# Query projections ahead of attention: a ring of five weight pairs, a rope table in scratch memory, three more query pairs made before the first score

## The chip, the core and the metric

One Trainium2 chip; the kernel runs on one of its cores. The metric is the device time of one execution in microseconds (us). Engines are named as in the profile: PE multiplies matrices, DVE works on vectors, ACT casts and applies functions, POOL works on vectors and issues DMAs, SP issues DMAs.

## The reference

A trunk of two layers over 1024 latent tokens and 256 context tokens, width 1024. Layer 0 mixes tokens with a convolution module, layer 1 with grouped-query attention; a SwiGLU feed-forward network (FFN) follows each. The changed part is the attention's input:

```python
qx = apply_rope(rmsnorm((hx @ wq).reshape(B, S, N_HEADS, HEAD_DIM), q_g), cos, sin)
kx = apply_rope(rmsnorm((hx @ wk).reshape(B, S, N_KV_HEADS, HEAD_DIM), k_g), cos, sin)
vx = (hx @ wv).reshape(B, S, N_KV_HEADS, HEAD_DIM)
...
s = jnp.einsum("bqkgd,bskd->bkgqs", qg, k).astype(jnp.float32) * (Dh ** -0.5)
p = jax.nn.softmax(s, axis=-1).astype(v.dtype)
o = jnp.einsum("bkgqs,bskd->bqkgd", p, v)
```

There are 16 query heads and 4 key heads of 64 each. Keys and values are those of 1024 latent and 256 context tokens, 1280 in all.

## The kernel before, in words

**Split operands.** Float32 products are made of halves: each operand is split in hi (rounded to float32r) and lo (the rest), and a product is three matmuls: hi with hi, lo with hi, hi with lo. For a weight of 128 x 1024 this is done in `wload` (L134 to L148): SP loads it (L141), ACT casts hi (L142), DVE (L146) or POOL (L148) subtracts lo; `lo_dve` sets the share of the two. The halves lie in pools of three, `wh` and `wl`, so a fourth weight's cast waits until the oldest one has been used up. The raw weights have buffers of their own (`wr0`, `wr1`, and room in `q`).

**Thirds.** The 1280 tokens are worked in three pieces: context (C), left latent (L, 512 tokens) and right latent (R, 512). The FFN of layer 0 is first run on C and L, then on R; as background of the latter the key and value of C are made. PE's products of two weights share the lines L165 to L167, or L176 to L178 for a first operand that is worked k by k.

**Projections for layer 1.** `qkv` (L802) is a generator that makes for one piece a key pair (hLk, hRk), values, and four query pairs (qL0 to qL3, qR0 to qR3). A pair is two 128-row results of 512 tokens, the even and odd halves of a rope rotation; `qk_pair` (L748 to L800) handles it. ACT squares both (L764, L765) and copies them scaled (L766, L767) into E and O, of which there are two sets, used in turn; PE sums the squares (L772, 16 small matmuls), DVE takes the reciprocal root (L775, L329 to L337). DVE then rotates: L790 writes both products with sin into `t12`, of which there is one, L791 to L793 do the rest. ACT casts the hi half into `t12` (L797) and POOL stores it from there to DRAM (`qsd`, L836; a key to `ksd`, L813); DVE makes the lo half in E and O (L799), and POOL stores that. A key has the root spread by PE (L783, L787) and multiplied in (L795) besides. All of it lies in the buffer `self.wk`, tile T5 of 4096 numbers a partition. The tables of cos and sin are loaded at the start of each `qkv` by two DMAs of POOL (L808, L809), for the left piece into HS.

In the order of the program: qkv of L begins (hLk, qL0, ...) as background work, beside it the last norm of FFN(0) on R and the first of layer 1 (L624, L627, L395, L401, on DVE, with sums on PE, L349, L363, L375); then hRk, qR0, and the rest of L. Which background step comes when is set by estimated costs (`pump`); a scheduler then orders each engine's queue, and every engine runs its own in that order.

**Attention.** Units are pairs of key head and tile of 128 queries, four query heads each. `scores` (L858 on) has PE write 128 x 1280 scores (L870), DVE scale them into one of several probability slots and take the minimum (L876), ACT exponentiate (L878). `values` transposes on PE (L888), casts (L891) and subtracts (L892) halves, ten times a unit, and multiplies by values (L894, L895). The first 16 units are for left queries (tiles 0 to 3), the next 16 for right ones. At the start of attention, three query pairs of the right piece are still to be made. They run as background of the first units; for as long, the score area has one place (`sring = [TOK]`) and two banks serve the projections. When they are done, T5 becomes three more probability slots and the score area has two places:

```python
for us in self.attn_stream(units, (self.kub, kbuf), dst(0), True):
    if self.bgq:
        self.pump(self.rate * us)
    elif pr4 is None:
        pr4 = self.T("T5", [P, 3, TOK])
        self.pring = self.pring[:4] + [pr4[:, 0], pr4[:, 1], pr4[:, 2]] + self.pring[4:]
        self.set_banks(**alone)
        self.sring = [0, TOK]
```

A tile such as T5 or HS, allocated anew, waits for all reads and stores of what lay there. In attention HS holds four probability slots (`prh`, "score area"); ahead of it, it holds the last operands of FFN(0) and then the table of the left piece, 1024 numbers of some 5120 a partition.

Of the kernel before, what the change touches and what calls it, by code (L numbers as in the profile page):

```python
# [8 lines left out]
F32 = mybir.dt.float32  # L9
F32R = mybir.dt.float32r  # L10
# [5 lines left out]
P = 128  # L16
# [3 lines left out]
SEQ = 1024  # L20
# [4 lines left out]
NH, NKV, HD = 16, 4, 64  # L25
# [29 lines left out]
class Kern:  # L55
    def __init__(self, tc, es, a):
        self.tc, self.nc, self.a = tc, tc.nc, a
        ep = es.enter_context
        self.cp = ep(tc.tile_pool(name="const", bufs=1))
        self.tp = ep(tc.tile_pool(name="sets", bufs=1))  # L60
        self.wp = ep(tc.tile_pool(name="w", bufs=3))
        self.sp = ep(tc.tile_pool(name="scr", bufs=3))
        self.pp = ep(tc.tile_pool(name="ps", bufs=1, space=bass.MemoryType.PSUM))
        self.dp = ep(tc.tile_pool(name="dr", bufs=1, space=bass.MemoryType.DRAM))
        self.ps = self.pp.tile([P, 8, 512], F32, tag="ps", name="ps")
        self.ring = {}
        self.set_banks(mm=[0, 1, 2], md=[3], st=[5, 6], cv=[4, 7])
        self.raws = [self.wp.tile([P, 1024], F32, tag=f"wr{i}", name=f"wr{i}", bufs=1) for i in range(2)]
        self.ri = 0
        self.bgq = []  # L70
        self.tie = None
        self.pre = []
        self.pace = 1
        self.rate, self.credit = 1.0, 0.0
        self.qk = 0
        self.share, self.lo_dve = 0.0, 0.0
# [58 lines left out]
    def wload(self, ap):  # L135
        nc = self.nc
        n = int(np.prod(ap.shape[1:]))
        raw = self.raw()[:, :n]
        hi = self.wp.tile([P, 1024], F32R, tag="wh", name="wh")[:, :n]
        lo = self.wp.tile([P, 1024], F32R, tag="wl", name="wl")[:, :n]  # L140
        nc.sync.dma_start(raw if len(ap.shape) == 2 else raw.rearrange("p (a b) -> p a b", a=ap.shape[1]), ap)  # L141
        nc.scalar.copy(hi, raw)  # L142
        self.share += self.lo_dve
        if self.share >= 1:
            self.share -= 1
            nc.vector.tensor_tensor(lo, raw, hi.bitcast(F32), op=ALU.subtract)  # L146
        else:
            nc.gpsimd.tensor_tensor(lo, raw, hi.bitcast(F32), op=ALU.subtract)  # L148
        return hi, lo
# [48 lines left out]
    def consts(self):  # L198
        nc, a = self.nc, self.a
        c = self.c = {}  # L200
        n = sum(int(np.prod(v)) for _, v in CONST)
        cst = self.cp.tile([P, n], F32, tag="cst", name="cst")
        nc.scalar.dma_start(cst, a["cst"])
        o = 0
        for k, v in CONST:
            w = int(np.prod(v))
            c[k] = cst[:, o:o + w]
            if len(v) > 1:
                names = "abc"[:len(v)]
                c[k] = c[k].rearrange("p (%s) -> p %s" % (" ".join(names), " ".join(names)), **dict(zip(names, v)))  # L210
            o += w
        self.x1d = a["x1d"] if "x1d" in a else self.dp.tile([P, KT, TOK], F32, tag="x1d", name="x1d")
        self.x2d = a["x2d"] if "x2d" in a else self.dp.tile([P, KT, TOK], F32, tag="x2d", name="x2d")
        self.x3d = a["x3d"] if "x3d" in a else self.dp.tile([P, KT, SEQ], F32, tag="x3d", name="x3d")
        self.qsd = a["qsd"] if "qsd" in a else self.dp.tile([NKV, P, 4, SEQ], F32, tag="qsd", name="qsd")
        self.ksd = a["ksd"] if "ksd" in a else self.dp.tile([NKV, HD, 2, TOK], F32, tag="ksd", name="ksd")
        self.od = self.dp.tile([P, KT, SEQ], F32, tag="od", name="od")

        self.vc = [self.dp.tile([CG, P, NC_], F32, tag=f"vc{k}", name=f"vc{k}") for k in range(KT)]
        self.vl = [self.dp.tile([CG, P, NL], F32, tag=f"vl{k}", name=f"vl{k}") for k in range(KT)]  # L220
        cs = self.cp.tile([P, KT, 2], F32, tag="cs", name="cs")
# [580 lines left out]
    def qkv(self, h, col0, n, wk, rope=None):  # L802

        nc, a, c = self.nc, self.a, self.c
        x = self.pairs(*h)
        lat0 = col0 - CTX
        if rope is not None:
            nc.gpsimd.dma_start(rope[:, 0, :n], a["cos"][:, lat0:lat0 + n])  # L808
            nc.gpsimd.dma_start(rope[:, 1, :n], a["sin"][:, lat0:lat0 + n])  # L809

        def ksink(i, v):
            for e in range(2):
                nc.gpsimd.dma_start(self.ksd[:, 32 * e:32 * e + 32, i, col0:col0 + n], v[:, e])  # L813
        pe, po = self.bank("mm"), self.bank("mm")
        self.projs((pe, po), a["wk"], x, n)
        self.qk_pair(pe, po, n, c["kg"], rope, wk, ksink)
        yield 5.0
        wv = [self.wload(a["wv"][q]) for q in range(2)]
        for j in range(n // P):
            out = self.bank("mm")  # L820
            self.mm3(out,
                     self.pairs(*h, j * P, (j + 1) * P),
                     lambda k: tuple(w[:, (k % 4) * 256:(k % 4 + 1) * 256] for w in wv[k // 4]),
                     KT, 256)
            jj = col0 // P + j
            ov = out[:, :256].rearrange("p (h d) -> p h d", d=HD)
            vh, vl = self.vst[:, :, jj, 0:HD], self.vst[:, :, jj, HD:P]
            nc.scalar.copy(vh, ov)
            nc.vector.tensor_tensor(vl, ov, vh.bitcast(F32), op=ALU.subtract)
            yield 0.5  # L830
        if rope is not None:
            for t in range(NKV):
                def qsink(i, v):
                    for e in range(2):
                        r = 64 * i + 32 * e
                        nc.gpsimd.dma_start(self.qsd[t, r:r + 32, :, lat0:lat0 + n].rearrange("d h t -> h d t"),  # L836
                                            v[:, e])
# [107 lines left out]
    def build(self):  # L945
        nc, a, c = self.nc, self.a, None
        self.consts()
        c = self.c
        hs = {b: [] for b in PIECES}
# [154 lines left out]
        def early():  # L1104
            yield from final(0, zv["C"][0], self.x1d, self.x2d, *PIECES["C"], 0, "KB")
            yield from final(0, zv["L"][0], self.x1d, self.x2d, *PIECES["L"], 0, "KB")
            yield from self.norm_in(1, None, (None, "T2", "T2"), 0, CTX, hC, xt=zv["C"][0][0])
            self.vst = self.T("HR", [P, NKV, NJ, P], F32R)
            self.rq = [self.cp.tile([P, SEQ // P * 4], F32, tag=f"rq{t}", name=f"rq{t}") for t in range(NKV)]
            wk = self.T("KB", [P, 8, 256])  # L1110
            yield from self.qkv(hC[0], 0, CTX, wk)
            yield from self.norm_in(1, None, (None, "T3", "T2"), CTX, CTX + 512, hL, xt=zv["L"][0][0])
            self.wk = self.T("T5", [P, 8, 512])
        self.raws.append(self.room())
        self.set_banks(mm=[0, 1, 2, 3], st=[5, 6], cv=[4, 7])
        self.bgq.append(early())
        for us in self.ffn(0, [(fv["R"][0], 512)], ("T1",), ("HS",), (zv["R"],)):
            self.pump(0.5 * us)
        self.drain()
        rope = self.T("HS", [P, 2, 512])  # L1120
        self.bgq.append(self.qkv(hL[0], CTX, 512, self.wk, rope))
        self.pump(7)
        self.kub = self.T("KB", [P, 2 * TOK], F32R)
# [6 lines left out]
        qr = self.qkv(hR[0], CTX + 512, 512, self.wk, self.wk[:, 0:2])  # L1130
        next(qr)
        self.load_k(0, self.kub, CTX + 512, TOK)
        for _ in range(5):
            next(qr)
        self.drain()
        self.attention(final, qr)

    def attention(self, final, qr):
        nc, a, c = self.nc, self.a, self.c
# [3 lines left out]
        ptt = self.T("T2", [P, 4, 2, 512], F32R)  # L1143
        self.ptring = [(ptt[:, i, 0], ptt[:, i, 1]) for i in range(4)]
        self.ptslot = self.si = self.qi = 0
        del self.raws[2:]
        self.qroom = self.room()
        units = [(t, q) for t in range(NKV) for q in range(4)]

# [183 lines left out]
```

## Time and profile before

| | us |
|---|---|
| median of 3 runs (3049.22 to 3057.86) | 3055.4 |
| profiled execution | 3058.17 |
| its span | 3056.4 |
| projections, from the last matmul of FFN(0) to the first score read | 1495.8 to 1641.0 |
| three pairs beside attention's first units | 1640 to 1757 |
| one unit of attention alone | 14.7 |

The profile is of one execution. A busy PE is not PE at its peak: matmuls are pipelined, and the bar of one overlaps the next. What a line waits for is named by the profile with the last semaphore that came. A pair's rope line is found by tile T, its store by `qsd`.

### The profile page before, as it was taken

To read this page: it belongs to the slowest core of one execution; us is meant where nothing else is said; L and a number is where in the kernel's file an instruction comes from. 1 tells how busy PE (TensorE), PEld (TensorE's weight loads), DVE (VectorE), ACT (ScalarE), POOL (GpSimd) and SP (SyncE) were. 2 spreads that over 40 slices of the span, in tenths; PEclk is the share of its full clock that TensorE was granted. 3 is DMA by queue.
4 is the path that set the end of the run, shared out by engine and by line. 5 is a ranking of instruction groups with operands and counts; after the bars stand their busy time and mean duration, and the time that the engine had idled before them with its cause. 6 is when DMAs were issued, how large, how long until landed. Compare 5 with 4: busy or idle time off the path is not lost. (4 is left out here: it accounts for less than half of the span.)

```text
span 3056.4 us, 39302 instructions
## 1 busy us (share of the span) xinstructions
PE 2927.2 (96%) x15086; PEld 2438.8 (80%) x15086; DVE 1902.2 (62%) x3341; ACT 1207.4 (40%) x1981; POOL 261.1 (9%) x413
## 2 busy tenths in 40 slices
PE   7899969999999999999988999999999999999997
PEld 5788868888888888888877777777787778788886
DVE  5886777866566358333565899766666654743335
ACT  5222255432222234222333688645555542332222
POOL 0000000101112011000013111110000000100000
PEclk9999979999999999999989999989999999999999
DMA  6542424433346235333346311223223132443332
GB/s 236 147 122 75 122 76 138 159 114 126 119 156 198 67 105 157 105 97 97 126 134 151 88 45 47 92 70 90 72 69 86 58 135 95 148 136 97 97 93 66
DMA packets 140716, 336.96 MB, mean 110 GB/s; under 512 B 39920, under 2 KB 61424, under 8 KB 139376
## 3 DMA queue, kind: packets, MB, share of 16 engines
q1 hardware_dynamic: 76432, 221.94, 22.6%
q0 software_dynamic: 37984, 104.42, 11.5%
q10 hardware_dynamic: 26112, 8.10, 1.1%
q8 instruction: 118, 1.93, 0.3%
q14 instruction: 70, 0.57, 0.1%
HBM read 289.76 MB, written 39.19 MB: 108 GB/s over the span
## 5 line engine op out<-in xcount | busy, mean ns | idle before, releaser
L167 PE MATMUL ps<-T,wl 128*128 128x512 f32 (+1 forms) x2128 | 802.9, 378 | 11.8 <-DVE wl L146 11.8
L165 PE MATMUL ps<-T,wh 128*128 128x512 f32 (+1 forms) x2128 | 806.3, 380 | 6.9 <-ACT T L154 4.1
L166 PE MATMUL ps<-T,wh 128*128 128x512 f32 (+1 forms) x2064 | 777.9, 377 | 0.7 <-DVE T L157 0.7
L142 ACT CAST wh<-wr 128x1024 fp32r<-128x1024 f32 x296 | 310.8, 1050 | 796.8 <-PE ps L166 569.0
L146 DVE TENSOR_TENSOR wl<-wr,wh 128x1024 fp32r<-128x1024 f32 x288 | 352.0, 1223 | 311.5 <-ACT wh L142 307.1
L167 PEld LDWEIGHTS ps<-T,wl 128*128 128x128 f32 x2128 | 407.3, 192 | 85.9 <-DVE wl L146 14.1
L165 PEld LDWEIGHTS ps<-T,wh 128*128 128x128 f32 x2128 | 407.2, 192 | 79.7 <-ACT T L154 5.6
L166 PEld LDWEIGHTS ps<-T,wh 128*128 128x128 f32 x2064 | 395.5, 192 | 68.9 <-DVE T L157 2.0
L166 PE MATMUL ps<-HS,wh 128*128 128x512 f32 (+1 forms) x784 | 303.8, 388 | 0.0
L892 DVE TENSOR_TENSOR T<-ps,T 128x512 fp32r<-128x512 f32 x320 | 216.7, 686 | 110.9 <-ACT T L891 109.7
L167 PE MATMUL ps<-HS,wl 128*128 128x512 f32 (+1 forms) x720 | 278.9, 388 | 0.0
L165 PE MATMUL ps<-HS,wh 128*128 128x512 f32 (+1 forms) x720 | 278.7, 389 | 0.0
L891 ACT CAST T<-ps 128x512 fp32r<-128x512 f32 x320 | 185.9, 585 | 194.8 <-PE ps L888 172.8
L888 PE MATMUL ps<-cst,T 128*128 128x128 f32 x1100 | 192.2, 276 | 1.9 <-DVE T L892 1.8
L876 DVE TENSOR_SCALAR_CACHE_REDUCE T<-ps,rq 128x1280 f32<-128x1280 f32 x110 | 169.9, 1544 | 27.8 <-PE ps L870 23.0
L722 DVE TENSOR_TENSOR T<-ps,T 128x512 f32<-128x512 f32 (+1 forms) x168 | 110.3, 662 | 113.1 <-PE ps L167 112.2
L888 PEld LDWEIGHTS ps<-cst,T 128*128 128x128 f32 x1100 | 134.0, 142 | 49.0 <-DVE T L892 28.6
L878 ACT ACTIVATE T<-T,mn 128x1280 f32<-128x1280 f32 x110 | 150.4, 1367 | 57.1 <-DVE T L876 55.2
L166 PEld LDWEIGHTS ps<-HS,wh 128*128 128x128 f32 x784 | 147.5, 188 | 28.6 <-DVE HS L157 0.2
L697 DVE TENSOR_TENSOR sm<-sm,ps 128x256 f32<-128x256 f32 (+1 forms) x88 | 54.5, 619 | 181.4 <-PE ps L167 181.2
L870 PE MATMUL ps<-KB,q 128*128 128x512 f32 (+1 forms) x576 | 146.8, 374 | 14.2 <-DVE HS L876 9.9
L167 PEld LDWEIGHTS ps<-HS,wl 128*128 128x128 f32 x720 | 135.4, 188 | 27.0
(227 smaller groups left out, 4574.0 us busy)
## 6 DMA issues: line engine op xcount, KB each, us to landing
wr<-in_w SPq DMA_DIRECT2D x220, 512.0 KB, 3.5
q<-in_w SPq DMA_DIRECT2D x44, 512.0 KB, 3.5
wr<-in_pw SPq DMA_DIRECT2D x40, 512.0 KB, 3.6
HR<-in_wmodT POOLq DMA_DIRECT2D x56, 256.0 KB, 3.9
q<-in_wmodT POOLq DMA_DIRECT2D x56, 256.0 KB, 3.9
qsd<-T POOLq DMA_DIRECT2D x32, 256.0 KB, 10.7
q<-qsd POOLq DMA_DIRECT2D x32, 256.0 KB, 3.3
wr<-in_wo SPq DMA_DIRECT2D x16, 512.0 KB, 4.4
```

The lines of the kernel that those rows point to most:

```text
L142: nc.scalar.copy(hi, raw)
L146: nc.vector.tensor_tensor(lo, raw, hi.bitcast(F32), op=ALU.subtract)
L165: nc.tensor.matmul(out[:, :n], lhsT=wh, rhs=xh, start=k == 0, stop=False)
L166: nc.tensor.matmul(out[:, :n], lhsT=wh, rhs=xl, start=False, stop=False)
L167: nc.tensor.matmul(out[:, :n], lhsT=wl, rhs=xh, start=False, stop=k == nk - 1)
L722: nc.vector.tensor_tensor(yd, out[:, :c1 - c0], yd, op=ALU.add)
L870: nc.tensor.matmul(sc[:, k0:k0 + w], lhsT=q[:, h, :], rhs=kt[:, p * TOK + k0:p * TOK + k0 + w], start=p == 0, stop=p == 1)
L876: nc.vector.tensor_scalar(out=pt, in0=sc, scalar1=rq[:, h:h + 1], scalar2=None, op0=ALU.mult, op1=ALU.min, accum_out=mn)
L878: nc.scalar.activation(pt, pt, AF.Exp, bias=mn, scale=-1.0, accum_out=sums[:, 0, h:h + 1])
L888: nc.tensor.transpose(tp[:, h * P:(h + 1) * P], Ps[h][:, j * P:(j + 1) * P], c["ident"])
L891: nc.scalar.copy(ph, tp)
L892: nc.vector.tensor_tensor(pl, tp, ph.bitcast(F32), op=ALU.subtract)
```

## The change

Three edits.

First, the pools of three hi and lo halves become a list of three explicit pairs, `self.whl`, taken in turn by a running count. Behind FFN(0) on R, HS is allocated as five slabs of 1024 numbers; four of them are two more pairs, so the ring has five until attention begins, where it is cut back to three (`del ... self.whl[3:]`). The fifth slab is the rope table of the left piece.

Second, the tables of cos and sin are copied to one scratch tensor in DRAM by two DMAs of POOL, 512 KB each, so that a piece's table of both is one DMA of 512 KB in place of two of 256 KB.

Third, three more steps of the right piece's generator run before attention: qR1, qR2 and qR3 are made there, and the loop above finds no background work but the generator's end.

```diff
-        hi = self.wp.tile([P, 1024], F32R, tag="wh", name="wh")[:, :n]
-        lo = self.wp.tile([P, 1024], F32R, tag="wl", name="wl")[:, :n]
+        self.wi += 1
+        hi, lo = (t[:, :n] for t in self.whl[self.wi % len(self.whl)])
...
+        self.rope = self.dp.tile([P, 2, SEQ], F32, tag="rope", name="rope")
...
-            nc.gpsimd.dma_start(rope[:, 0, :n], a["cos"][:, lat0:lat0 + n])
-            nc.gpsimd.dma_start(rope[:, 1, :n], a["sin"][:, lat0:lat0 + n])
+            nc.gpsimd.dma_start(rope[:, :, :n], self.rope[:, :, lat0:lat0 + n])
...
             self.wk = self.T("T5", [P, 8, 512])
+            for i, t in enumerate(("cos", "sin")):
+                nc.gpsimd.dma_start(self.rope[:, i], a[t])
...
-        rope = self.T("HS", [P, 2, 512])
+        hs = self.T("HS", [P, 5, 1024], F32R)
+        rope = hs[:, 4].bitcast(F32).rearrange("p (i n) -> p i n", i=2)
+        self.whl += [(hs[:, i], hs[:, i + 1]) for i in (0, 2)]
...
         self.drain()
+        for _ in range(NKV - 1):
+            next(qr)
         self.attention(final, qr)
...
-        del self.raws[2:]
+        del self.raws[2:], self.whl[3:]
```

What moves in the queues. In the changed kernel a line behind L800 has a number larger by three, so L790 is L793 there, L142 is L144, L395 is L398 and L876 is L878; the numbers behind names tell allocations apart.

ACT where FFN(0) ends and the projections begin, before; `wh_11486` and `wh_11491` are the first two weights of the projections:

```order
L142 CAST wh_11438<-q_8935 128x1024
L696 ACTIVATE sm_11388<-ps_72 128x512
L142 CAST wh_11486<-wr0_73 128x1024
L154 CAST HS_8937<-sm_11389 128x512
L383 ACTIVATE acc_11394<-T1_8936 128x512
L386 ACTIVATE sb_11415<-T1_8936 128x512
L142 CAST wh_11491<-wr1_74 128x1024
```

The same place in the changed kernel:

```order
L144 CAST wh2_79<-q_8730 128x1024
L699 ACTIVATE sm_11049<-ps_72 128x512
L156 CAST HS_8732<-sm_11050 128x512
L386 ACTIVATE acc_11055<-T1_8731 128x512
...
L144 CAST wh2_79<-wr0_73 128x1024
L389 ACTIVATE sb_11137<-T1_8731 128x512
L144 CAST HS_11140<-wr1_74 128x1024
```

The last weight of FFN(0) lies in `wh2`; the next cast, the first of the projections, goes to `wh2` too, and the second to HS. Both now stand behind the reads of T1 by L389.

DVE at the norm of the right piece, before (L395 and L401 are the norm, L790 begins the rope of qL1):

```order
L337 SCALAR_TENSOR_TENSOR nr<-nq,nr 128x16
L779 TENSOR_SCALAR rq_9471<-nr 128x16
L395 SCALAR_TENSOR_TENSOR sb<-T_8936,col_8057,ps 128x512 x3
L401 SCALAR_TENSOR_TENSOR T_11833<-sb,mod_103,T_11832 128x512 x3
L395 SCALAR_TENSOR_TENSOR sb<-T_8936,col_8057,ps 128x512 x3
L401 SCALAR_TENSOR_TENSOR T_11833<-sb,mod_103,T_11832 128x512 x3
L395 SCALAR_TENSOR_TENSOR sb<-T_8936,col_8057,ps 128x512 x2
...
L790 TENSOR_TENSOR T_9937<-T_9937,HS 128x1024
```

In the changed kernel:

```order
L340 SCALAR_TENSOR_TENSOR nr<-nq,nr 128x16
L793 TENSOR_TENSOR T_9688<-T_9688,HS 128x1024
L398 SCALAR_TENSOR_TENSOR sb<-T_8731,col_7880,ps 128x512 x3
L404 SCALAR_TENSOR_TENSOR T_11481<-sb,mod_110,T_11480 128x512 x3
L398 SCALAR_TENSOR_TENSOR sb<-T_8731,col_7880,ps 128x512 x3
L404 SCALAR_TENSOR_TENSOR T_11481<-sb,mod_110,T_11480 128x512 x3
L398 SCALAR_TENSOR_TENSOR sb<-T_8731,col_7880,ps 128x512 x2
...
L794 TENSOR_TENSOR T_9688<-T_9688,HS 128x1024
```

The first rope product of qL1 stands ahead of the norm, the second still behind it.

DVE at the first scores of attention in the changed kernel, from the first product of qR3 (`T_12498` is T1, `T_12523` is T5):

```order
L793 TENSOR_TENSOR T_9688<-T_9688 128x1024
...
L794 TENSOR_TENSOR T_9688<-T_9688 128x1024
...
L878 TENSOR_SCALAR T_12498,mn<-ps,rq_9244 128x1280
...
L878 TENSOR_SCALAR HS,mn<-ps,rq_9244 128x1280
...
L802 TENSOR_TENSOR T_9688<-T_9688 128x1024
...
L878 TENSOR_SCALAR T_12498,mn<-ps,rq_9244 128x1280
...
L878 TENSOR_SCALAR HS,mn<-ps,rq_9244 128x1280
...
L878 TENSOR_SCALAR T_12523,mn<-ps,rq_9244 128x1280
L901 RECIPROCAL sums<-sums 128x4
L894 TENSOR_TENSOR T_12500<-ps,T_12500 128x512
```

In before the first score (L876) stands between qL2 and qL3, and the four products L790 of qL3, qR1, qR2 and qR3 lie between the scores of the first units; now all of them stand ahead of the first score, and the fifth score is written to T5, where the pairs' buffers lay.

More of the change, by code (lines that the diff above doesn't have):

```diff
@@ L68, in __init__ @@
         self.raws = [self.wp.tile([P, 1024], F32, tag=f"wr{i}", name=f"wr{i}", bufs=1) for i in range(2)]
-        self.ri = 0
+        self.ri = self.wi = 0
+        self.whl = [tuple(self.wp.tile([P, 1024], F32R, tag=f"{t}{i}", name=f"{t}{i}", bufs=1) for t in ("wh", "wl"))
+                    for i in range(3)]
         self.bgq = []
```

## The prediction

> **What bounds the kernel now.** I read the page's totals first, then a table of stretches around the place that changes, then the waits there.
>
> ```profile
> span 3056.4 us, 39302 instructions
> PE 2927.2 (96%) x15086; PEld 2438.8 (80%) x15086; DVE 1902.2 (62%) x3341; ACT 1207.4 (40%) x1981; POOL 261.1 (9%) x413
> ```
> ```profile
> core 0: us, PE busy (x) PEld busy (x) DVE busy (x) ACT busy (x) POOL busy (x), PEclk, DMA share, GB/s
> 5.00:42.00 37.00, 26.82 (x168) 17.68 (x169) 18.43 (x60) 17.10 (x48) 0.00 (x0) 0.86 1.03 399
> 1495.00:1640.00 145.00, 131.61 (x724) 113.91 (x723) 91.08 (x205) 53.72 (x79) 29.57 (x40) 0.91 0.48 132
> 1640.00:1757.00 117.00, 103.71 (x525) 81.72 (x523) 83.28 (x160) 65.82 (x101) 30.30 (x36) 0.90 0.46 111
> 1757.00:1904.00 147.00, 143.18 (x860) 117.55 (x860) 134.12 (x220) 119.34 (x200) 20.71 (x33) 1.00 0.17 46
> ```
>
> PE is busy almost throughout, but the projections (1495 to 1640) and the mixed stretch of three query pairs and the first attention units (1640 to 1757) leave 13 us each idle and run at a clock of 0.9. Attention alone (from 1757) has the full clock, and DVE works 134 of 147 us: it is the limit there. This gives the pace of one unit:
>
> ```profile
> L892 DVE TENSOR_TENSOR T<-ps,T 128x512 fp32r<-128x512 f32 x100 | 66.7, 685 | 10.4 <-ACT T L891 10.1
> ```
>
> 100 subtractions at ten a unit (one for each 128 keys of 1280) are ten units in 147 us, 14.7 us a unit. What stops the projections stands in the waits of DVE, 1580 to 1745, and of PE, 1490 to 1740:
>
> ```profile
> DVE T L790 <- DMA qsd<-T: 27.4, 4, 10.1
> ```
> ```profile
> PE ps L787 <- DVE sm L783: 6.0, 1, 6.0
> PE ps L167 <- DVE wl L146: 3.8, 1, 3.8
> ```
>
> DVE waits 27.4 us for stores of queries, PE only 3.8 us for a weight's lo half. So in front of attention the chain is not the weights. It is this, from one pair to the next:
>
> ```profile
> 1614.95 1.22 DVE L790 TENSOR_TENSOR T<-T 128x1024 f32<-128x1024 f32 x1 [1.69 <-DMA ksd<-T]
> 1632.10 2.09 DVE L790 TENSOR_TENSOR T<-T,HS 128x1024 f32<-128x1024 f32 x1 [6.14 <-DMA qsd<-T]
> 1648.26 1.22 DVE L790 TENSOR_TENSOR T<-T,HS 128x1024 f32<-128x1024 f32 x1 [4.37 <-DMA qsd<-T]
> 1665.16 1.22 DVE L790 TENSOR_TENSOR T<-T 128x1024 f32<-128x1024 f32 x1 [10.08 <-DMA qsd<-T]
> ```
> ```profile
> 1652.22 1.05 ACT L797 CAST T<-T 128x1024 fp32r<-128x1024 f32 x1 [2.41 <-DVE T L793]
> ```
> ```profile
> 1653.57 1.48 POOL L836 DMA_DIRECT2D qsd<-T  x2 [7.94 <-ACT T L797]
> ```
> ```profile
> qsd<-T POOLq DMA_DIRECT2D x32, 256.0 KB, 10.7
> ```
>
> A pair's first rope product (L790) goes into t12, the only buffer of its kind, which the pair before still stores its hi half from. 1648.26: product; 1652.22: cast into t12; 1653.57: POOL issues the store; it lands about 10.7 us later; 1665.16: the next product. From 1614.95 to 1665.16 are three periods, **16.7 us** each. PE's own work of a pair is less:
>
> ```profile
> 1601.60:1630.00 28.40, 28.40 (x142) 24.00 (x141) 11.75 (x25) 10.08 (x15) 10.68 (x13) 1.00 0.64 148
> ```
> ```profile
> L772 PE MATMUL ps<-cst,sm 128*128 128x4 f32 x32 | 3.8, 242 | 0.0
> ```
> ```profile
> 1495.56 0.39 PE L167 MATMUL ps<-HS,wl 128*128 128x512 f32 x1
> 1495.79 0.39 PE L176 MATMUL ps<-T,wh 128*128 128x512 f32 x1
> 1496.24 0.39 PE L178 MATMUL ps<-T,wl 128*128 128x512 f32 x1
> ```
>
> Large matmuls start 0.23 us apart (the last fence); the 142 of the gapless stretch are 110 large and 32 small, so a small one costs (28.4 - 110 x 0.23) / 32 = 0.1 us. A pair has 48 large and 16 small: 12.6 us.
>
> **The change, part by part.** Times are those of before unless said otherwise. Sums are made against the profiled run, 3058.2 us, 2.8 above the median of 3055.4.
>
> *Rope copies: +2.6.* Two copies of 512 KB in DRAM stand at the head of POOL's queue and wait for nothing. In 5 to 42 us all DMA engines are busy (share 1.03, 399 GB/s), and PE waits there for its first operands. 1.05 MB at 0.40 MB/us is 2.6 us; bounds: 0, if the copies get only gaps, and 5, as each byte is read and written. I take the middle, since no row has a copy from DRAM to DRAM. Two rope loads that become one are not on the chain: nothing. Six lo splits go from POOL to DVE, 1.2 us each: into the 27.4 us that DVE waits, nothing; without that cover 7.
>
> *The seam: +3.3.* The first weight of the projections now takes the pair that the FFN's last weight holds, and the second takes HS, also read by the FFN's last matmuls. Both casts, done in before at 1484.66 and 1490.37, must wait for PE's 1495.6:
>
> ```profile
> 1484.66 1.05 ACT L142 CAST wh<-wr 128x1024 fp32r<-128x1024 f32 x1 [3.95 <-PE ps L166]
> 1490.37 1.05 ACT L142 CAST wh<-wr 128x1024 fp32r<-128x1024 f32 x1
> 1496.01 1.04 ACT L142 CAST wh<-q 128x1024 fp32r<-128x1024 f32 x1
> ```
> ```profile
> 1498.29 1.22 DVE L146 TENSOR_TENSOR wl<-q,wh 128x1024 fp32r<-128x1024 f32 x1
> ```
>
> The cast of 1496.01 waited for the same matmul; its lo half was there at 1499.5. If the first weight comes like that, L178 goes at 1499.5 and not 1496.24: 3.3. Bounds 1.3 (only the cast, ending at 1497.05, counts) and 4.5 (the second one queues behind).
>
> *DVE's order at the norm of the right third: +4.7.* Product L790 (now L793) of pair qL1 stands behind that norm in before, ahead of it now.
>
> ```profile
> 1562.21 2.06 DVE L395 SCALAR_TENSOR_TENSOR sb<-T,col,ps 128x512 f32<-128x512 f32 x3 [0.23 <-PE ps L375]
> 1573.23 1.22 DVE L790 TENSOR_TENSOR T<-T,HS 128x1024 f32<-128x1024 f32 x1
> ```
> ```profile
> 1580.63 1.08 ACT L797 CAST T<-T 128x1024 fp32r<-128x1024 f32 x1
> ```
> ```profile
> 1557.39 2.88 POOL L836 DMA_DIRECT2D qsd<-T  x4 [13.42 <-ACT T L797]
> ```
>
> It waits for qL0's store: 1557.4 + 3.3 + 10.7 = 1571.4. Only then, 1.2 later, comes the norm, in before 1562.2 to 1573.2, 11.0 long. After it stand 6.2 us of the rope (1573.23 + 1.22 to 1580.63), less one lo split (1.2) that now stands elsewhere. L797 of qL1: 1571.4 + 1.2 + 11.0 + 5.0 = 1588.6, in place of 1580.6: 8.0 with the seam. Bounds for this term: 0 (the store lands before 1562) and 6. *The key pair hRk: +2.0*, since two halves of rope (0.7 each) and a split (1.2) now stand ahead of its L783 and L795, less what PE's transposes hide. Bounds 0 and 3. The stall of 3.8 us on a lo half goes, but on PE, which this chain does not wait for. **Slip: 10.0.**
>
> *Three pairs in front: from interleaved to in series.*
>
> ```profile
> 1640.98 1.55 DVE L876 TENSOR_SCALAR_CACHE_REDUCE T<-ps,rq 128x1280 f32<-128x1280 f32 x1 [1.21 <-PE ps L870]
> 1765.66 1.54 DVE L876 TENSOR_SCALAR_CACHE_REDUCE T<-ps,rq 128x1280 f32<-128x1280 f32 x1
> ```
>
> Unit 0's first score is read at 1640.98, unit 5's at 1765.66: from there on before and after do the same in the same order, so that point carries the result. After: qL3's cast at 1652.2 + 10.0 = 1662.2; three periods of 16.7 put qR3's product at 1662.2 + 50.1 - 4.0 = 1708.3 (4.0 from product to cast, above). The first score stands behind it and a second product in DVE's queue: 1710.9. The fifth goes into T5, where the pairs' buffers lie: it waits until qR3's lo store has landed. Two scores (1.5 each), two splits (1.2 each) and two sums (0.7 each, as L892 above) stand up to that half, which puts the store's issue at 1718.1, its landing at 1728.8. This is unit 1's first score; DVE has unit 0's L892 queued behind it. Four units of 14.7 then give 1787.6 for unit 5: **+21.9**, the slip in it. If that landing were hidden, unit 1 would begin some 8 us earlier.
>
> *The clock.* PE would idle 4.1 us of each 16.7 in front. Two idles of the trace, of 7.6 and 3.8 us, and the clock around them:
>
> ```profile
> 1670.68 0.58 PE L870 MATMUL ps<-KB,q 128*128 128x256 f32 x1 [7.56 <-DVE HS L876]
> 1557.37 0.79 PE L167 MATMUL ps<-T,wl 128*128 128x512 f32 x1 [3.85 <-DVE wl L146]
> ```
> ```profile
> 1553.80:1560.60 6.80, 3.23 (x8) 2.56 (x9) 6.80 (x19) 1.05 (x1) 2.83 (x4) 0.50 0.27 78
> 1666.50:1676.70 10.20, 6.02 (x16) 4.75 (x17) 10.04 (x19) 5.10 (x7) 5.09 (x5) 0.50 0.43 112
> ```
>
> Half clock for 6.8 us costs PE 3.4: 12.6 + 3.4 = 16.0, still under 16.7, nothing. For 10.2 us it costs 5.1: 17.7, so 1.0 a pair, 3 in all; I take nothing and keep 3 for the range. The Trainium skill, TensorE: Matmul & The Clock Gate, "What's actually happening", has PE's clock at half after an idle window of about 3.4 us, and at full again after as long a busy one; by that every gap of 4.1 could bring it, and each stretch would be short, so its sum stays with the first row's. Both rows agree that such gaps halve the clock; the second shows a longer stretch than the rule's single window.
>
> Sum: 2.6 + 21.9 = 24.5 on 3058.2 is 3082.7; less 2.8, **3080 us**.
>
> **Rivals.** (A) is the above, 3080, by its bounds 3069 (seam 1.3, norm, key pair and copies 0) to 3089 (clock 3, copies 5, seam 4.5, key pair 3, norm 6).
> (B) *No slip, only series and ramp*: splits moved from POOL to DVE and earlier weights make up for seam and norm. 21.9 - 10.0 + 2.6 = +14.5: 3070. For it: five pairs of buffers end the 3.8 stall; against: the chain runs through the store.
> (C) *The stores land sooner*, as no attention traffic is beside them, period 14.7 from qL1 on (1580.6) with the slip: 1580.6 + 7 x 14.7 + 16.5 + 58.8 = 1758.8, -6.9, with 10.0 and 2.6 +5.7: 3061, no change. The 16.5 are from qR3's cast to unit 1's first score, above. Against it: the 16.7 were themselves measured mostly with little traffic (1615 to 1648).
> (D) *The other side: weights, not stores, bound the front.* Then the ring of five lets all seven pairs from 1580.6 run at PE's 12.6, without slip: 1580.6 + 88.2 + 16.5 + 58.8 = 1744.1, -21.6 + 2.6 = -19.0: 3036. For it: PE idles 13 us in 1495 to 1640, and ran without a gap where weights came in time (1601.6 to 1630); against: 27.4 us of DVE's waits name the store. It decides where the products stand less than 14 us apart.
>
> **How the numbers follow.** A 0.58, B 0.16, C 0.13, D 0.13. About 0.3% (9 us) is what a measurement of this kernel can tell from no change: A and B are slower (B at 3070 by 15), C the same, D faster; a tenth of B falls into the same. Slower 0.73, same 0.14, faster 0.13. The range 3050 to 3090 leaves out D and a little of A; the likeliest alone has 3069 to 3089.
>
> **What would show it.** In after: a gap of about 3 us on PE at the seam, products (L793) 16 to 17 us apart down to qR3, first score read near 1711, none of the fifth kind until about 1729, unit 5 near 1788; behind it everything as before, 22 to 25 us later. Products closer than 14 us, or a first score before 1690, make it wrong; so does time that comes from the weights' ring elsewhere.

## The result, and the profile after

The changed kernel takes 3088.3 us (median of 6 runs, 3082.5 to 3097.0), the kernel before 3050.8 us (6 runs, 3047.4 to 3057.9): a ratio of **1.0121, 95% interval 1.0102 to 1.0140**, 31 to 43 us slower. The forecast was slower by 24.5 us, with 3080 us and a range of 3050 to 3090. The direction and the chain hold; the size is one and a half times the forecast. Both profiled executions lie above their kernel's median (after, 3097.0 us, by 8.7; before, 3058.2, by 7.4), so the spans differ by 38.8 us where the medians differ by 37.5. I read the traces up to unit 5 of attention, where the forecast was made, and then what follows it.

The page's head and the stretches, of after (columns as before: PE, PEld, DVE, ACT, POOL, clock, DMA share, GB/s):

```profile
span 3095.2 us, 39307 instructions
PE 2930.1 (95%) x15086; PEld 2442.1 (79%) x15086; DVE 1906.7 (62%) x3347; ACT 1208.2 (39%) x1981; POOL 247.0 (8%) x407
```
```profile
1495.00:1640.00 145.00, 125.10 (x679) 108.57 (x678) 88.56 (x191) 53.77 (x77) 21.36 (x33) 0.87 0.48 132
1640.00:1718.00 78.00, 56.62 (x263) 45.89 (x262) 34.57 (x86) 17.79 (x25) 13.74 (x20) 0.90 0.52 119
1718.00:1760.00 42.00, 28.95 (x140) 22.17 (x140) 29.59 (x53) 25.53 (x39) 5.09 (x8) 0.77 0.22 54
1795.00:1942.00 147.00, 143.08 (x861) 117.44 (x860) 134.26 (x220) 119.21 (x201) 21.05 (x34) 1.00 0.17 46
```

PE's work is the same, 15086 matmuls. It idles 20 us in the 145 of the projections (13 before), 21 us in the 78 in which the front pairs are made, and 13 us in the 42 of attention's ramp. From 1795 on attention alone has the rates of before. DVE's waits from 1580 to 1745 in after, the first with the longest single wait at the end:

```profile
DVE T L793 <- DMA qsd<-T: 45.9, 6, 11.6
DVE T L878 <- DMA qsd<-T: 8.9, 1, 8.9
```

27.4 us of waiting for the stores of queries have become 45.9, and 8.9 at a score. The rows of DVE themselves, from qL3's first product to unit 1's first score, and unit 5's:

```profile
1666.69 1.22 DVE L793 TENSOR_TENSOR T<-T,HS 128x1024 f32<-128x1024 f32 x1 [11.63 <-DMA qsd<-T]
1684.53 1.22 DVE L793 TENSOR_TENSOR T<-T 128x1024 f32<-128x1024 f32 x1 [6.93 <-DMA qsd<-T]
1699.83 1.23 DVE L793 TENSOR_TENSOR T<-T 128x1024 f32<-128x1024 f32 x1 [8.59 <-DMA qsd<-T]
1715.85 1.23 DVE L793 TENSOR_TENSOR T<-T 128x1024 f32<-128x1024 f32 x1 [6.33 <-DMA qsd<-T]
1718.36 1.54 DVE L878 TENSOR_SCALAR_CACHE_REDUCE T<-ps,rq 128x1280 f32<-128x1280 f32 x1
...
1738.85 1.55 DVE L878 TENSOR_SCALAR_CACHE_REDUCE T<-ps,rq 128x1280 f32<-128x1280 f32 x1 [8.93 <-DMA qsd<-T]
...
1798.53 1.54 DVE L878 TENSOR_SCALAR_CACHE_REDUCE T<-ps,rq 128x1280 f32<-128x1280 f32 x1
```

Three pairs in series, 49.2 us from 1666.69 to 1715.85; then the first score; then the fifth, which waits for T5. Unit 5 starts at 1798.53, before it was 1765.66: 32.9 us later, where the forecast had 24.5 with the copies.

Unit 5 doesn't carry the whole result, though. These are the first scores of units 15 and 20, in before and then in after:

```profile
1912.09 1.54 DVE L876 TENSOR_SCALAR_CACHE_REDUCE T<-ps,rq 128x1280 f32<-128x1280 f32 x1
2097.31 1.55 DVE L876 TENSOR_SCALAR_CACHE_REDUCE T<-ps,rq 128x1280 f32<-128x1280 f32 x1 [1.02 <-PE ps L870]
```
```profile
1944.95 1.54 DVE L878 TENSOR_SCALAR_CACHE_REDUCE T<-ps,rq 128x1280 f32<-128x1280 f32 x1
2134.11 1.55 DVE L878 TENSOR_SCALAR_CACHE_REDUCE T<-ps,rq 128x1280 f32<-128x1280 f32 x1 [1.43 <-PE ps L872]
```

The difference is still 32.9 us at unit 15, and 36.8 at unit 20, behind the change from left to right queries. The prediction has before and after do the same in the same order from unit 5 on. They don't: T5's slots come into use at the fifth score now, and so the units up to 15 write their scores to the tiles in another order than in before (unit 1's four go to T, H, H, T in before, with H for HS, and to T, T, T, T in after).

The place of the slip in after: the issue of qL0's store on POOL, its wait on DVE with the norm behind, and qL1's cast on ACT:

```profile
1560.77 2.87 POOL L838 DMA_DIRECT2D qsd<-T  x4 [12.15 <-ACT T L800]
```
```profile
1574.54 1.23 DVE L793 TENSOR_TENSOR T<-T,HS 128x1024 f32<-128x1024 f32 x1 [5.63 <-DMA qsd<-T]
1575.68 2.06 DVE L398 SCALAR_TENSOR_TENSOR sb<-T,col,ps 128x512 f32<-128x512 f32 x3
```
```profile
1592.03 1.05 ACT L800 CAST T<-T 128x1024 fp32r<-128x1024 f32 x1
```

PE's waits from 1490 to 1600 in after show who suffered:

```profile
PE ps L178 <- ACT T L403: 7.5, 1, 7.5
...
PE ps L178 <- ACT wh L144: 1.1, 1, 1.1
PE ps L178 <- ACT HS L144: 0.7, 1, 0.7
```

The late casts of the seam cost PE 1.8 us. The 7.5 us are the key pair hRk, which waits for the norm that waits for the store.

### The profile page after: what moved, and what is told of

It is laid out like the page before. It is cut to its first block, busy times and chain, and to the rows that moved or that the text cites. A ratio compares the mean times of both kernels' runs of the same rounds, so it can differ in the third digit from the quotient of the medians.

```text
span 3095.2 us, 39307 instructions
## 1 busy us (share of the span) xinstructions
PE 2930.1 (95%) x15086; PEld 2442.1 (79%) x15086; DVE 1906.7 (62%) x3347; ACT 1208.2 (39%) x1981; POOL 247.0 (8%) x407
## 5 line engine op out<-in xcount | busy, mean ns | idle before, releaser
L167 PE MATMUL ps<-T,wh 128*128 128x512 f32 (+1 forms) x2072 | 780.0, 377 | 10.1 <-ACT T L156 7.6
L169 PE MATMUL ps<-T,wl 128*128 128x512 f32 (+1 forms) x2072 | 778.5, 376 | 8.4 <-DVE wl L148 8.4
L168 PE MATMUL ps<-T,wh 128*128 128x512 f32 (+1 forms) x2008 | 752.8, 375 | 0.7 <-DVE T L159 0.7
L144 ACT CAST wh<-wr 128x1024 fp32r<-128x1024 f32 x287 | 301.2, 1050 | 780.4 <-PE ps L168 555.9
L169 PEld LDWEIGHTS ps<-T,wl 128*128 128x128 f32 x2072 | 394.7, 191 | 79.8 <-DVE wl L148 10.8
L167 PEld LDWEIGHTS ps<-T,wh 128*128 128x128 f32 x2072 | 394.4, 191 | 79.9 <-ACT T L156 9.1
L168 PEld LDWEIGHTS ps<-T,wh 128*128 128x128 f32 x2008 | 382.4, 190 | 66.7 <-DVE T L159 2.0
L878 DVE TENSOR_SCALAR_CACHE_REDUCE T<-ps,rq 128x1280 f32<-128x1280 f32 x112 | 172.9, 1543 | 33.3 <-PE ps L872 20.3
## 6 DMA issues: line engine op xcount, KB each, us to landing
qsd<-T POOLq DMA_DIRECT2D x32, 256.0 KB, 11.1
```

The costliest lines, as they stand in the source:

```text
L167: nc.tensor.matmul(out[:, :n], lhsT=wh, rhs=xh, start=k == 0, stop=False)
L168: nc.tensor.matmul(out[:, :n], lhsT=wh, rhs=xl, start=False, stop=False)
L169: nc.tensor.matmul(out[:, :n], lhsT=wl, rhs=xh, start=False, stop=k == nk - 1)
L878: nc.vector.tensor_scalar(out=pt, in0=sc, scalar1=rq[:, h:h + 1], scalar2=None, op0=ALU.mult, op1=ALU.min, accum_out=mn)
```

## The experiments

The differences in the table are the ratio to the kernel before, run on the same chip in the same call, times its median of some 3051 us, with the 95% interval.

| kernel | median us | ratio | difference us |
|---|---|---|---|
| after, all three edits | 3088.3 | 1.0121 | +37 (31 to 43) |
| e_front, third edit alone | 3074.2 | 1.0067 | +20 (15 to 26) |
| e_ring_rope, first and second | 3070.5 | 1.0059 | +18 (13 to 22) |
| e_rope, second alone | 3058.1 | 1.0019 | +6 (2 to 9) |
| e_seam, after with the ring turned | 3088.6 | 1.0132 | +40 (34 to 47) |
| e_late, after with T5 later | 3078.6 | 1.0086 | +26 (22 to 31) |
| e_front_t12, two t12 | 3044.1 | 0.9978 | -7 (-10 to -3) |
| e_front_t12_late | 3034.0 | 0.9949 | -16 (-19 to -12) |
| e_t12, before with two t12 | 3039.3 | 0.9965 | -11 (-15 to -6) |
| e_front16, other store order | 3034.9 | 0.9948 | -16 (-20 to -12) |
| e_after16 | 3039.2 | 0.9967 | -10 (-14 to -6) |
| e_before16 | 3039.9 | 0.9959 | -13 (-17 to -8) |
| e_front16_t12 | 3026.8 | 0.9923 | -23 (-29 to -19) |

There are ten pairs, in the order hLk, qL0, qL1, hRk, qR0, qL2, qL3, qR1, qR2, qR3. The next table has the first products of the last six as the traces have them, in us, the first score read, and unit 1's and unit 5's first:

| kernel | qR0 | qL2 | qL3 | qR1 | qR2 | qR3 | score 1 | unit 1 | unit 5 |
|---|---|---|---|---|---|---|---|---|---|
| before | 1615.0 | 1632.1 | 1648.3 | 1665.2 | 1687.3 | 1707.0 | 1641.0 | 1681.1 | 1765.7 |
| after | 1627.9 | 1645.5 | 1666.7 | 1684.5 | 1699.8 | 1715.8 | 1718.4 | 1738.8 | 1798.5 |
| e_front | 1608.7 | 1628.5 | 1648.7 | 1668.2 | 1686.2 | 1705.5 | 1708.0 | 1726.4 | 1786.0 |
| e_front_t12 | 1599.1 | 1611.8 | 1624.8 | 1637.6 | 1650.4 | 1663.2 | 1665.7 | 1684.1 | 1744.5 |
| e_front16 | 1610.9 | 1622.9 | 1637.7 | 1650.5 | 1663.5 | 1676.2 | 1678.7 | 1690.3 | 1748.7 |
| e_t12 | 1598.5 | 1611.8 | 1631.2 | 1644.4 | 1670.2 | 1689.5 | 1626.9 | 1664.0 | 1747.9 |

### The edits apart

The third edit alone is the kernel before with two lines more:

```diff
         self.drain()
+        for _ in range(NKV - 1):
+            next(qr)
         self.attention(final, qr)
```

> The kernel before with the third edit alone: three more query pairs made in front, ring of three, no scratch copy. DVE's order at the norm of the right third is that of before. Theory A (the one store buffer t12 sets the pairs' pace; the slip belongs to the ring): products L790 some 16.5 us apart down to the last pair, first score near 1700 us, the fifth near 1719, +10 to +16 us on the kernel before. Rival B (all of the loss comes from making the pairs in front): +30 us or more. Rival C (all of the loss comes from the ring): within 5 us of before.

+20 us, above what my theory gave and far from either rival. The products stand 18 to 20 us apart, not 16.5, although the score came late for the reason named. A wait row of DVE, 1580 to 1745, and the issue row of the stores from 1560 to 1700, both of e_front:

```profile
DVE T L790 <- DMA qsd<-T: 45.4, 6, 9.2
```
```profile
qsd<-T POOLq DMA_DIRECT2D x24, 256.0 KB, 12.3
```

The stores land in 12.3 us (median), and DVE waits for them as long as in after. Why they land later here than on before's page (10.7) no run settles; below, one such store is compared with its traffic.

The first and second edits without the third are after with those two lines taken out.

> The first two edits alone: ring of five in HS and scratch copy, the pairs as background of attention as in before. Theory A (slip by the late first casts, by DVE's order at the norm and by the key pair): product of pair qL1 near 1574, cast of hRk near 1614 in place of 1601, +10 to +20 us on before. Rival B (loss from the pairs in front alone): within 4 us of before, or faster by up to 4, since PE's stall of 3.8 us on a lo half goes. Rival C (loss from the ring alone): +30 us or more.

+18 us, as theory A has it; its first product of qL1 is at 1569.8 and the cast of hRk at 1610.6, some 4 us ahead of the times expected. The two halves add up: 20 + 18 against 37 for all.

The second edit alone, as in the change's diff:

> The second edit alone: the scratch copies of cos and sin and one load in place of two. Theory A: 1 to 3 us, seen on PE within the first 60 us and kept to the end. Rival (it fits the gaps): 0, with PE's first matmuls at the times of before.

+6 (2 to 9). PE's early matmuls are 1.6 to 3.0 us later than before from 50 to 370 us, but of this nothing is left at 700 us, and down to attention's last score its trace is level with before (0.5 us later). Of the 4.5 us by which its span is longer 4.0 come behind that score, where all kernels do the same work and their traces take 598.1 to 602.8 us. So the time has a cost clear of noise, the trace doesn't show it as one of the copies, and where it lies stays open.

The seam, mended: the ring is turned when it grows, so that the first cast goes to the pair used longest ago.

```diff
-        self.whl += [(hs[:, i], hs[:, i + 1]) for i in (0, 2)]
+        k = (self.wi + 1) % 3
+        self.whl = self.whl[k:] + self.whl[:k] + [(hs[:, i], hs[:, i + 1]) for i in (0, 2)]
+        self.wi = -1
```

> The changed kernel with the ring turned when it grows to five, so that the first weight of the projections takes the pair used longest ago, as in before; DVE's order at the norm stays that of the changed kernel (product of pair qL1 ahead of the norm). Theory A (the slip is mostly the wait at the norm and what follows it): PE's waits for the first two casts (1.9 us) go, 0 to 4 us faster than the changed kernel, the wait of PE for the norm stays at some 8 us. Rival (the late casts cause most of the slip): 10 us or more faster than the changed kernel.

No gain (3088.6 and 3088.3 us). PE's two waits for casts are gone from its trace, and the wait for the norm is longer, in PE's waits from 1490 to 1600:

```profile
PE ps L178 <- ACT T L403: 8.1, 1, 8.1
```

So mending the seam gains nothing, though its waits are gone; with an interval of 34 to 47 us against 31 to 43 a gain of the waits' 1.8 us could not be told from none.

### The stores

Two buffers t12 in turn, the second in HS and given up where attention begins, otherwise e_front:

```diff
-        E, O, t1, t2 = (wk[:, i, :n] for i in (o, o + 1, 6, 7))
-        EO, t12 = wk[:, o:o + 2, :n], wk[:, 6:8, :n]
+        E, O = (wk[:, i, :n] for i in (o, o + 1))
+        EO, t12 = wk[:, o:o + 2, :n], self.t12s[self.qk % len(self.t12s)][:, :, :n] if n == 512 else wk[:, 6:8, :n]
+        t1, t2 = t12[:, 0], t12[:, 1]
...
-        rope = self.T("HS", [P, 2, 512])
+        hs = self.T("HS", [P, 4, 512])
+        rope = hs[:, 0:2]
+        self.t12s = [hs[:, 2:4], self.wk[:, 6:8]]
```

> The third edit alone as in e_front, with two buffers t12 used in turn (the second lies in HS), so that a pair's first product no longer waits for the store of the pair just before. Theory A (the store of t12 sets the pace): products 12.5 to 14.5 us apart in front of attention, first score at 1675 to 1690 in place of some 1700, 10 to 22 us faster than e_front, that is -8 to +4 on the kernel before. Rival (weights of a ring of three, or PE's order, set the pace): products stay 15.5 to 17 us apart and the time is within 4 us of e_front's.

By the table 27 us faster than e_front (30 by the medians), more than I had expected, and 7 faster than before. DVE's rows of e_front_t12 (L791 is the first product there):

```profile
1624.82 1.23 DVE L791 TENSOR_TENSOR HS<-T,HS 128x1024 f32<-128x1024 f32 x1
1637.60 1.22 DVE L791 TENSOR_TENSOR T<-T 128x1024 f32<-128x1024 f32 x1
1650.41 1.23 DVE L791 TENSOR_TENSOR HS<-T 128x1024 f32<-128x1024 f32 x1
1663.20 1.23 DVE L791 TENSOR_TENSOR T<-T 128x1024 f32<-128x1024 f32 x1
```

No waits, 12.8 us apart: PE's pace, which the prediction worked out as 12.6. A ring of three feeds it. So the single t12 set the pace.

Then the landing itself. In the kernel before, a store of 128 rows goes to DRAM as four groups (`[4, 32 of 128, ...]`, head first). In e_front16 the queries lie head by head within each quarter, so that the 128 rows go out in sequence; a load of queries pays with four DMAs for one:

```diff
-self.dp.tile([NKV, P, 4, SEQ], F32, tag="qsd", name="qsd")
+self.dp.tile([NKV, 4, P, SEQ], F32, tag="qsd", name="qsd")
...
-                        r = 64 * i + 32 * e
-                        nc.gpsimd.dma_start(self.qsd[t, r:r + 32, :, lat0:lat0 + n].rearrange("d h t -> h d t"),
-                                            v[:, e])
+                        nc.gpsimd.dma_start(self.qsd[t, 2 * i + e, :, lat0:lat0 + n], v[:, e])
...
-        nc.gpsimd.dma_start(q, self.qsd[t, :, :, qt * P:(qt + 1) * P])
+        for j in range(4):
+            nc.gpsimd.dma_start(q[32 * j:32 * j + 32],
+                                self.qsd[t, j, :, qt * P:(qt + 1) * P].rearrange("(h d) t -> d h t", h=4))
```

> The third edit alone as in e_front, one buffer t12, but queries lie in DRAM in another order, so that a store of 128 rows goes out as 128 rows in sequence rather than as four groups (a load of queries is four DMAs in place of one). Theory A (how long a store takes to land sets the pace): products 12.5 to 14.5 us apart, qsd<-T lands in 3 to 6 us, time within 6 us of e_front_t12's, so -10 to +2 on before. Rival (the second buffer helped by something else than by hiding the landing): spacing and time as in e_front, +20.

-16 on before, with one t12. The page's issue row of e_front16 against 11.1 us in after, and two of its products:

```profile
qsd<-T POOLq DMA_DIRECT2D x32, 256.0 KB, 4.8
```
```profile
1650.48 1.22 DVE L790 TENSOR_TENSOR T<-T 128x1024 f32<-128x1024 f32 x1
1663.45 1.23 DVE L790 TENSOR_TENSOR T<-T 128x1024 f32<-128x1024 f32 x1
```

13.0 us apart, no wait. It beats e_front_t12 (3044.1) by 9 us. One of the reasons is in the table of products: unit 1's first score comes 12 us after score 1, not 18, since the store that T5 waits for lands early too. (Unit 5's place in the table can't be compared between these two to a few us: the profiled execution of e_front16, span 3041.5, is among its longer ones, that of e_front_t12, 3040.3, among its shorter ones.) Two kernels with different cures, one for the buffer and one for the landing, agree that the landing behind t12 is the bound.

The same store order in the changed kernel:

> The changed kernel with the same order of queries in DRAM. Theory A (the slip comes from a product that waits for a store while DVE's norm and the key pair stand behind it): with stores that land early the slip goes but for the seam's 2 us and the copies' 1; within 6 us of e_front16. Rival (the ring itself costs: late casts, PE waits for weights, order): 12 to 20 us slower than e_front16.

4 us behind e_front16 by the medians and 6 by the ratios, with intervals that overlap: at the edge of theory A's 6, and short of the rival's 12 to 20. The two edits that cost 18 us with stores in four groups cost some 4 to 6 with 128 rows in sequence. PE's wait for the norm, 7.5 us in after, is this in e_after16 (PE's waits, 1490 to 1600):

```profile
PE ps L178 <- ACT T L403: 1.8, 1, 1.8
```

The casts of the seam still cost 1.8 us there.

And in the kernel before:

> The kernel before with the order of queries in DRAM of e_front16 and nothing else: pairs beside attention as in before, ring of three, one t12. Theory A: also here the stores no longer bind, -10 to -20 on before; if it equals e_front16 within 4 us, making the pairs in front is worth nothing by itself once stores land early. Rival (in front, with two score places from the start, the pairs cost less): 5 to 12 us slower than e_front16.

-13 (-17 to -8). e_front16 is at -16 (-20 to -12): the intervals overlap, so making pairs in front is worth 3 us or nothing once stores land early. All three edits against e_before16 are e_after16's -10 against -13: what costs 37 us with stores in four groups costs 3 or nothing with 128 rows in sequence. That is the plainest sign that the stores are what the change loses by. For e_t12 the difference to the kernel before is the diff of two t12 above, cut back to one (`del self.t12s[0]`) where attention begins:

> The kernel before with two buffers t12 until attention begins and one from there on; nothing else. Theory A: the pairs ahead of attention come 12.6 to 14 us apart where PE has no other work, the first score some 10 us earlier than 1641; three pairs beside attention keep their single buffer: -4 to -12 on before. Rival (in the kernel before the stores are hidden by other work of PE): within 3 us of before. Whether making the pairs in front is worth something by itself, once stores no longer bind, is told by e_front_t12 against this one.

-11, in the expected range, first score at 1626.9. Beside it e_front_t12 has -7: making the pairs in front gained nothing there either.

### The ramp

After with T5's slots taken into use 19 steps into attention:

```diff
-        for us in self.attn_stream(units, (self.kub, kbuf), dst(0), True):
+        self.drain()
+        self.set_banks(**alone)
+        self.sring = [0, TOK]
+        for step, us in enumerate(self.attn_stream(units, (self.kub, kbuf), dst(0), True)):
             if self.bgq:
                 self.pump(self.rate * us)
-            elif pr4 is None:
+            elif pr4 is None and step > 18:
```

> The changed kernel, but the three probability slots of T5 are taken into use only in unit 1's second half (19 steps into attention), so that no early score waits for the pairs' last store. Both score places are used from the start. Theory A: the 8.9 us for which DVE waited at the fifth score go; 7 to 10 us faster than the changed kernel, so +27 to +31 on before. Rival (the wait covers another one, of PE or of probability slots in use): within 3 us of the changed kernel, +35 to +39.

+26: some 10 us faster than after. That this is near the 8.9 us of the wait is in part chance. In the traces 6.6 us of it lie between the first score and unit 1's (13.9 us for 20.5), 1.0 is lost again up to unit 5, and 3.9 lie between units 15 and 20: that stretch takes 185.2 us in e_late, whose scores go to the tiles in the order of before, and 185.2 in before, but 189.2 in after and 189.3 in e_front. So the ramp's term was real, and taking T5's slots early cost once more, where the prediction had nothing. The size of the second cost is rough: over all kernels here the stretch is 184.9 to 189.3 us with the slots early and 182.6 to 186.7 in the order of before. The same edit on e_front_t12:

> e_front_t12 with the probability slots of T5 taken into use only in unit 1's second half, as in e_late. Theory A: the 7.4 us for which DVE waits at the fifth score go: 5 to 9 us faster than e_front_t12, -12 to -16 on before. Rival (another wait takes its place): within 2 us of e_front_t12.

-16, some 10 us faster than e_front_t12, slightly more than its wait of 7.4 us. Beside e_t12 (-11) the three pairs in front are now 5 us ahead; the intervals overlap.

Both cures of the stores together, third edit, ring of three, no copies:

> e_front16 with two buffers t12 besides. Theory A: PE sets the pace of the pairs already, within 4 us of e_front16. Rival (the landing of some 5 us still costs at each pair): 5 to 10 us faster.

**3026.8 us, 0.9923 (0.9906 to 0.9939), 19 to 29 us faster than before**: the rival's time, faster than e_front16 by some 8 us, but not for the rival's reason. In its trace the products are 12.7 to 13.0 us apart from qR0 on, where e_front16 has 12.0 to 14.8; from qR0 to qR3 that is 64 us for 65. What goes is one wait ahead of them, of e_front16's qR0, for the store of the key pair hRk, whose order in DRAM the edit left as it was:

```profile
1610.89 1.22 DVE L790 TENSOR_TENSOR T<-T 128x1024 f32<-128x1024 f32 x1 [6.70 <-DMA ksd<-T]
```

With two t12 no product waits for a store, and unit 5 starts at 1741.1 in place of 1748.7. It is the fastest of all kernels here.

## Why the prediction was right, and where its size was off

**The chain.** Right, and shown from two sides: store of t12, product, cast, store. Taking the wait away by a second buffer or by a faster store brought the products from 18 to 20 us apart down to 13 and turned +20 into -7 and -16.

**The three pairs in series.** Right in after: 49.2 us for 50.1. No loss by the clock shows in them, as I took it, though the clock was 0.90 in that stretch. In e_front the same three took 56.8: the hi halves that the products wait for landed 12.6 to 13.9 us after their issue there, 9.9 to 12.4 in after.

**The ramp.** Right in kind: the fifth score waited 8.9 us for T5's last store, and e_late took 6.6 us off there. From qR3's product to unit 1's score it was 23.0 us for 20.5.

**Attention behind it.** Right up to unit 5: four units in 59.7 us for 58.8. Wrong behind it: the difference there was put at nothing, but unit 15 to unit 20 took 3.9 us more, as T5's slots came early (e_late, above).

**The seam.** Too high: 1.8 us for PE, and 2.2 us at qL0's cast (1559.4 against 1556.1, less the 1.1 of the copies) for 3.3; and mending it gained nothing (e_seam).

**The copies.** In after's trace PE is 1.1 us late ahead of the projections, for 2.6, but in those of the other kernels with copies that I compared there (e_rope, e_ring_rope, e_late, e_after16, e_seam) it is 1.0 to 5.2 us early; e_rope's time says 6 (2 to 9). Not settled.

**The step that failed is the landing of a store, put at 10.7 us everywhere.** It was the median of the whole page; the forecast's own example had 11.6 (store issued at 1653.57, product at 1665.16). qL0's store was issued at 1560.77 and the product that waited for it began at 1574.54: 13.8 us, and 3.1 of the 3.3 us by which the norm's term (8.0 for 4.7) is too small lie there. The change did not make that store slower. The rows of the four stores of qL0, in before (issued from 1557) and in after (from 1560):

```profile
qsd<-T POOLq DMA_DIRECT2D x4, 256.0 KB, 13.1
```
```profile
qsd<-T POOLq DMA_DIRECT2D x4, 256.0 KB, 12.6
```

So the number to take stood in the trace of before. qL2's store is the other place. In before it was issued at 1638.27 and the product began 10.0 us later, and the forecast moved that step unchanged. In after it had this on POOL and on SP's queue around it:

```profile
1650.85 1.37 POOL L838 DMA_DIRECT2D qsd<-T  x2 [14.17 <-ACT T L800]
...
1654.68 1.08 POOL L851 DMA_DIRECT2D T<-ksd  x2
```
```profile
1651.16 3.64 SPq L143 DMA_DIRECT2D wr<-in_wo  x2
```

It took 15.8 us up to the product at 1666.69: 4.5 us of slip that no term had. The load of keys (two of 640 KB) followed it in before too; the two weights (512 KB each) did not, and in e_front, where 1.0 MB of weights moved beside it, the four stores of qL2 landed in 14.5 us (median), for 10.7 in before. That the weights slow it is what the traces suggest; no run takes them away. With these, the hRk term (2.6 for 2.0), the ramp's 2.5 and 0.9 of attention, less 2.5 of seam and copies together and 0.9 of the series, 24.5 becomes the 32.9 at unit 5 but for 0.1. With the 3.9 behind unit 15 it is 36.8, which is near the 37 of the medians.

**What of this is one execution.** e_late and after have the same order of work on PE, DVE and ACT from the projections to the first score, and e_seam differs by the turned ring and by what the scheduler made of it. Yet their first scores are at 1707.6 and 1702.5 where after has 1718.4. The first four rows are the slip against before's trace that each step adds, the last one is a length, all in us:

| term | forecast | after | e_late | e_seam |
|---|---|---|---|---|
| up to qL0's cast (copies, seam) | 5.9 | 3.4 | -3.9 | -9.9 |
| to qL1's cast (the norm) | 4.7 | 8.0 | 7.8 | 8.2 |
| to hRk's cast (key pair) | 2.0 | 2.6 | 2.6 | 2.0 |
| to qL3's product | 0 | 4.5 | 0.5 | 2.6 |
| length of qL3 to qR3 | 50.1 | 49.2 | 49.8 | 50.1 |

The norm, the key pair and the series repeat, and in all three traces qL0's store has 12.6 us or more up to its product. What comes ahead of qL0 and the size at qL2 do not repeat: after's 4.5 us there is the largest of three. One reason ahead of qL0 is PE's clock. From 1546 to 1556 us, in after and then in e_late:

```profile
1546.00:1556.00 10.00, 10.00 (x37) 8.95 (x38) 0.08 (x1) 2.00 (x3) 1.08 (x2) 0.50 0.56 212
```
```profile
1546.00:1556.00 10.00, 9.43 (x57) 8.19 (x55) 6.21 (x24) 4.35 (x6) 2.42 (x4) 1.00 0.43 162
```

The same queue ran at half clock in one execution and at full clock in the other, 37 matmuls for 57, and after's trace fell 6 us behind e_late's there. So the sum for unit 5 closes on one execution of each kernel, and that it closes to 0.1 is in part luck. By the medians the change's parts stand like this: the third edit alone was forecast at 11.9 us (21.9 less the slip of 10.0) and cost 20, the first and second were forecast at 12.6 (10.0 and 2.6) and cost 18. Both halves cost 1.4 to 1.7 times their forecast, so none made up for the other.

**The signs.** First score at 1718 (forecast near 1711), fifth at 1739 (1729), unit 5 at 1798.5 (1788), products of the front pairs 15.3 to 17.8 us apart (16 to 17). Each is in its order and 7 to 11 us late in after's trace; in e_late's the first score, at 1707.6, is ahead of the forecast. "Everything as before" behind unit 5 did not come (36.8 us late at unit 20), nor the gap of 3 us on PE at the seam (1.8).

**The rivals.** (B), no slip, fell: e_ring_rope alone has 18 us. (C), stores that land sooner, fell the other way: 11.1 us on the page for 10.7. (D), weights as the bound, fell: the ring of three runs at 12.8 us a pair with two t12.

## What to carry to other kernels

Work that is moved out of the cover of another phase runs at the pace of its slowest recycled buffer, so before it is moved its period should be read from the trace (here 16.7 us, against 12.6 of PE) and the store behind that buffer looked at first. A deeper ring for an operand that nobody waits for gains nothing, and it can still cost through the order in which a scheduler then puts a waiting instruction ahead of other work. A page's median is not the landing of a given store: qL0's had 13.1 us in the trace of before, against a median of 10.7, and qL2's went from 10.0 to 15.8 with other transfers beside it. And a point from which "all goes on as before" has to be checked in the order of buffers too, not in the order of work alone.

## What the runs showed of the hardware

How a store's rows are grouped set its time here more than its size or its company. From 1689 to 1701 in after four stores (one pair's) have the DMA engines to themselves, and from 1656 to 1664 in e_front16 four stores of the same size run together with loads of queries. First after:

```profile
DMA packets 1057, 1.01 MB, mean 84 GB/s; under 512 B 813, under 2 KB 813, under 8 KB 1057
qsd<-T POOLq DMA_DIRECT2D x4, 256.0 KB, 9.9
```

Then e_front16:

```profile
DMA packets 497, 1.43 MB, mean 179 GB/s; under 512 B 147, under 2 KB 147, under 8 KB 497
qsd<-T POOLq DMA_DIRECT2D x4, 256.0 KB, 2.6
```

With four outer groups the same 256 KB land in 9.9 us (median of the four, the first of them in 6.9); as 128 rows in sequence they land in 2.6 us (the first in 2.3). The data move in packets of 4096 bytes in both. Of the 813 packets under 512 B in after's stretch 752 have 8 bytes, which e_front16 doesn't have, and the rest 4, like e_front16's 147; the 752 take 6.3 us of engine time in all, beside 74 for the data. What differs is how many data packets are open at once: 3 or 4 in after while its first store moves alone (1691.25 to 1693 us) and up to 13 with all four, but 12 to 17 in e_front16 as its first two begin (1657.75 to 1658.25). The Trainium skill, DMA: Bandwidth & Descriptors, "Why a DMA increments its semaphore by 16 and not by 1", says that a DMA is spread over the largest number of engines up to 16 that divides the slowest dimension, on both sides, with an exception for some direct copies. By that four groups use 4 engines and 128 rows use 16, a factor of four, and 9.9 to 2.6 and the open packets agree with it; no run here names the engines that moved a store.
